# Sums over partitions by VectorE's 32x32 transposes instead of products with ones, in a hybrid attention and recurrence layer

## The chip, the cores and the metric

The kernel runs on one core of one Trainium2 chip. The metric is the device time of one execution in microseconds (us); several runs are taken and their median is given. In the profile PE is TensorE (PEld its weight loads), DVE is VectorE, ACT is ScalarE, POOL is GpSimd and SP is SyncE, which issues the transfers here.

## The reference

One decoder layer over 512 tokens of width 1024, in float32: x is normalised, one wide projection feeds a block-sparse attention branch (8 heads of 64) and a gated linear recurrence (4 heads of 128), and both are projected up, gated, merged and added to x. Two normalisations matter here, that of x over its 1024 channels and that of each recurrence head's output over its 128 channels:

```python
def rmsnorm(x, gain):
    xf = x.astype(jnp.float32)
    return xf * lax.rsqrt(jnp.mean(xf * xf, axis=-1, keepdims=True) + RMS_EPS) * gain.astype(jnp.float32)
...
xn = rmsnorm(h, norm_gain[i]).astype(dt)
proj = xn @ w_in[i]
aq, ak, av, ag, bq, bf, bi, bg, gate_a, gate_b = jnp.split(proj, split_pts, axis=-1)
...
yb = hgrn2_chunkwise(qb, kb, vb, log_f)
yb = rmsnorm(yb, hgrn_out_gain[i].reshape(HGRN_HEADS, HGRN_VDIM)).reshape(b, s, HGRN_WIDTH)
```

## The kernel before

**Layout.** x and the heads' outputs lie with channels on the 128 partitions and the 512 tokens on the free axis. x is eight tiles `xr0` to `xr7` of 128x512. A sum over channels is therefore a sum over partitions.

**Products.** To keep float32's precision, each operand is split into a high and a low part (`split`: ScalarE copies the high part, VectorE subtracts), and each product is three (`mm3`, line 256, and `proj_tok`, line 391). A weight matrix comes in pieces of 128x1024 (`wf`), each split into `wh` and `wl` (lines 239 and 240) two pieces ahead of use.

**Order.** TensorE runs in the order of the program. The main line is the list of projections: `bi` and `av` (values of the recurrence and of the attention, from x without its norm, `gh` and `gl`), then, with the normalised `xh` and `xl`, `bf0` and `bq0` (forget gate and query of recurrence head 0), `aq`, `ak`, and from `ORDER` the rest: `bg` and `ag` (gates), `bf`/`bq` 1 to 3, `gb` and `ga` (merge gates). The recurrence and the attention are generators that are woven into it: a counter `now` adds up an assumed cost of the products, and `yield 3.5` means that the generator goes on when 3.5 us more of products have been written. The order on VectorE, ScalarE, GpSimd and SyncE is set by a scheduler at build time, which takes what is marked with high priority sooner; each of these engines too runs its list strictly in order.

**x's norm.** While `bi` runs, the squares of the eight tiles are added into `ssum`. `x_norm` splits it, two products with `onesd` (1/1024 everywhere) put the mean of squares of each token on all partitions (`mp`), `rsqrt` takes the inverse root (logarithm and exponential on ScalarE, one step of Newton on VectorE, lines 267 to 272), and `xr` is scaled by it (line 355, three tiles on GpSimd). Four transposes (`mt`) turn it so that tokens are on partitions (`rt`), for the values.

**A recurrence head.** `hgrn_gates` prepares the gates; `hgrn_intra` prepares operands on VectorE and ScalarE (`hx`, `hkx`, `hqx`, last `near`, lines 463 to 465) and then has TensorE form the scores in small products (`lpb`, `lpa`); `hgrn_out` forms chunk states (`hktp`, `hds`, `st`) and the output (`hop`). Then comes the norm: the square `ht`, its split `hth` and `htl`, a pause of 3.5 us of products, two products with `ones128` (`hms`), `rsqrt`, and the scaling (line 609). The next head's `hgrn_intra` follows 3.1 us of products later, if its gates are there.

Of the kernel before, what the change touches and what calls it, by code (L numbers as in the profile page):

```python
# [12 lines left out]
R = mybir.dt.float32r  # L13
I32 = mybir.dt.int32
AF = mybir.ActivationFunctionType
OP = mybir.AluOpType
AX = mybir.AxisListType

S = 512
D = 1024  # L20
KD = D // 128
NT = S // 128
# [14 lines left out]
XN = 3.0  # L37
# [13 lines left out]
AHEAD = 150  # L51
# [6 lines left out]
def hybrid_layer_kernel(  # L58
# [16 lines left out]
    V, A, G, PE = nc.vector, nc.scalar, nc.gpsimd, nc.tensor  # L75

    cst = ctx.enter_context(tc.tile_pool(name="cst", bufs=1))
# [4 lines left out]


    BUFS = {"w": 2, "wh": 3, "wl": 3, "A": 16, "R": 4, "X": 16, "YB": 8, "H": 10, "T": 3, "Q": 4, "QM": 2, "QX": 2, "KT": 2, "P": 4, "PT": 2,
            "PT0": 2, "PT2": 2, "SG": 4, "YS": 1, "VV": 8, "s32": 1, "st": 1, "ps": 8}

    def unit(tag, name, dt=F32, shape=(128, 512)):
        return sb.tile(list(shape), dt, tag=tag, bufs=BUFS[tag], name=name)

    def bank(tag, name):  # L90
        return psum.tile([128, 512], F32, tag=tag, bufs={"mm": 4, "g": 2, "a": 2}[tag], name=name)
# [34 lines left out]
    def cost(us):  # L126
        now[0] += us
# [17 lines left out]
    one = nc.const_aps.tensor(1.0, (128, 128), F32)  # L145
    for i in range(WARM):
        PE.matmul(warm[:, 0:128], one, one, start=True, stop=True)
    onesd = cst.tile([128, 128], R, name="onesd")
    A.activation(onesd, one, AF.Copy, scale=1.0 / D)
    ones128 = cst.tile([128, 128], R, name="ones128")  # L150
    A.activation(ones128, one, AF.Copy, scale=1.0 / 128)
    epsc = cst.tile([128, 1], F32, name="epsc")
    V.memset(epsc, EPS)
    onec = cst.tile([128, 1], F32, name="onec")
# [1 line left out]
    ident = cst.tile([128, 128], F32, name="ident")  # L156
# [6 lines left out]
    ogain = sm[:, 10:14]  # L163
# [28 lines left out]
    def split(hi, lo, src):  # L192
        A.activation(hi, src, AF.Copy)
        V.tensor_tensor(lo, src, hi.bitcast(F32), op=OP.subtract)

    def scale_split(hi, lo, src, g):
        A.activation(hi, src, AF.Copy, scale=g)
        V.scalar_tensor_tensor(lo, src, g, hi.bitcast(F32), op0=OP.mult, op1=OP.subtract)
# [65 lines left out]

    def rsqrt(y, t, ms):

        A.activation(t, ms, AF.Ln, bias=epsc[:, 0:1])
        A.activation(y, t, AF.Exp, scale=-0.5)
        V.scalar_tensor_tensor(t, ms, EPS, y, op0=OP.add, op1=OP.mult)
        V.tensor_tensor(t, t, y, op=OP.mult)  # L270
        V.tensor_scalar(t, t, -0.5, 1.5, op0=OP.mult, op1=OP.add)
        V.tensor_tensor(y, y, t, op=OP.mult)
# [17 lines left out]
    rt = cst.tile([128, NT], F32, name="rt")  # L290
# [24 lines left out]
    ssum = unit("YB", "ssum")  # L315

    def x_square(k):
# [4 lines left out]
        A.activation(t, xr[k], AF.Square)  # L322
        V.tensor_tensor(ssum, ssum, t, op=OP.add)

    def x_norm():
        th = unit("YB", "ssh", R)
        tl = unit("YB", "ssl", R)
        with tc.high_priority(offset=AHEAD):
            split(th, tl, ssum)
        yield XN  # L330
        rstd = unit("YB", "rstd")
        with tc.high_priority(offset=AHEAD):
            x_normalise(th, tl, rstd)
        yield RT

        mt = bank("g", "mt")
        for t in range(NT):
            PE.transpose(mt[:, t * 128:t * 128 + 128], rstd[:, t * 128:t * 128 + 128], ident)
        cost(0.44)
        with tc.high_priority(offset=AHEAD):  # L340
            A.activation(rt, mt.rearrange("p (t n) -> p t n", t=NT)[:, :, 0], AF.Copy)
        for t in range(NT):
            A.activation(vb[t], vb[t], AF.Copy, scale=rt[:, t:t + 1])

    def x_normalise(th, tl, rstd):
        mp = bank("g", "mp")
        PE.matmul(mp, onesd, th, start=True, stop=False)
        PE.matmul(mp, onesd, tl, start=False, stop=True)
        cost(0.46)
        tmp = unit("YB", "rtmp")  # L350
        rsqrt(rstd, tmp, mp)
        with tc.manual_schedule(engines={mybir.EngineType.DVE}):
            def scaled(k):
                if k < KD and k not in ONPOOL:
                    V.scalar_tensor_tensor(xr[k], xr[k], gain[:, k:k + 1], rstd, op0=OP.mult, op1=OP.mult)
            for k in ONPOOL:
                G.tensor_tensor(xr[k], xr[k], rstd, op=OP.mult)
            scaled(0)
            scaled(1)
            for k in range(KD):  # L360
                h_ = unit("X", f"xh{k}", R)
                l_ = unit("X", f"xl{k}", R)
                if k in ONPOOL:
                    scale_split(h_, l_, xr[k], gain[:, k:k + 1])
                else:
                    split(h_, l_, xr[k])
                xh.append(h_)
                xl.append(l_)
                scaled(k + 2)


    def proj_tr(i, name):
        ws = weight(w_tr[i])
        ps = bank("mm", name)
        mm3(ps, ws[0], ws[1], xh, xl, KD)
        return ps
# [186 lines left out]
    def hgrn_out(h, vb):  # L563
        kb, qm, cum, kd = hg[h][:4]
        nk = 3 * 128
        yield 5.0
        kt = bank("g", f"hktp{h}")
        for c in range(3):
            PE.transpose(kt[:, c * 128:c * 128 + 128], kd[:, c * 128:c * 128 + 128], ident)
        cost(0.33)  # L570
        kts = unit("KT", f"hkt{h}", shape=(128, 3 * 128))
        A.activation(kts[:, :nk], kt[:, :nk], AF.Copy)
        yield 2.5
        hv = slice(h * 128, h * 128 + 128)
        dsp = bank("g", f"hds{h}")
        for c in range(3):
            PE.matmul(dsp[:, c * 128:c * 128 + 128], kts[:, c * 128:c * 128 + 128], vb[c][:, hv],
                      start=True, stop=True)
        cost(0.65)
        st = unit("st", f"st{h}", shape=(128, 3, 128))  # L580
        V.tensor_copy(st[:, 0], dsp[:, 0:128])
        for c in (1, 2):
            e = c * 128 + 127
            V.scalar_tensor_tensor(st[:, c], st[:, c - 1], cum[:, e:e + 1], dsp[:, c * 128:c * 128 + 128],
                                   op0=OP.mult, op1=OP.add)
        yield 3.0
        op_ = bank("g", f"hop{h}")
        for c in range(NT):
            s_ = slice(c * 128, c * 128 + 128)
            PE.matmul(op_[:, s_], vb[c][:, hv], sc[:, c, :], start=True, stop=(c == 0))  # L590
            if c:
                PE.matmul(op_[:, s_].rearrange("p (g t) -> p g t", t=32), st[:, c - 1], qm[:, 4 * c:4 * c + 4, 0:32],
                          start=False, stop=True)
        cost(1.5)
        o = unit("YB", f"ho{h}")
        y = unit("Q", f"hy{h}")
        t = unit("Q", f"ht{h}")
        th = unit("Q", f"hth{h}", R)
        tl = unit("Q", f"htl{h}", R)
        with tc.high_priority(offset=AHEAD):  # L600
            A.activation(t, op_, AF.Square)
            split(th, tl, t)
        yield 3.5
        ms = bank("g", f"hms{h}")
        PE.matmul(ms, ones128, th, start=True, stop=False)
        PE.matmul(ms, ones128, tl, start=False, stop=True)
        cost(0.43)
        rsqrt(y, t, ms)
        V.scalar_tensor_tensor(o, op_, ogain[:, h:h + 1], y, op0=OP.mult, op1=OP.mult)
        hg[h] += (o,)  # L610

    def hgrn_gated(h, sbg, res):
# [9 lines left out]
    def recurrence(vb, sbg, res):  # L622
        for h in range(GH):
            yield lambda: h in hg
            if h == 0:
                yield H0
            yield from hgrn_intra(h)
            yield from hgrn_out(h, vb)
            spawn(hgrn_gated(h, sbg, res))
            yield HP  # L630
# [215 lines left out]
    with tc.manual_schedule(engines=FIRST):  # L846
        bi = proj_tok(2, "bi", gh, gl, start)
    vb = values(bi, "bi")
    spawn(x_norm())
    va = values(proj_tok(3, "av", gh, gl), "av", rt)  # L850
    spawn(recurrence(vb, sbgs, yb))
# [11 lines left out]
    def up(i, n, ys, name):  # L863
        ws = weight(w_up[n, i])
        ps = bank("mm", name)
        mm3(ps, ws[0], ws[1], [y[0] for y in ys], [y[1] for y in ys], 4)
        return ps
# [3 lines left out]
    for kind, i in ORDER:  # L871
# [6 lines left out]
        elif kind == "ub":  # L878
            drain(f"yb{GH - 1}")
            ps = up(1, i, yb, f"ub{i}")  # L880
            V.tensor_tensor(sg["gb", i], ps, sg["gb", i], op=OP.mult)
        else:
            ps = proj_tr({"ga": 16, "gb": 24}[kind] + i, f"{kind}{i}")
# [3 lines left out]
    for n in range(KD):  # L887
        ga, gb = sg["ga", n], sg["gb", n]
        drain(f"ya{HPAIRS - 1}")
        ps = up(0, n, ya, f"ua{n}")  # L890
# [9 lines left out]
    for n in range(KD):  # L900
# [3 lines left out]
        ps = bank("mm", f"h{n}")  # L904
        mm3(ps, ws[0], ws[1], mh, ml, KD)
        t = unit("H", f"hf{n}")
# [8 lines left out]
    for k in range(2):  # L915
        t = unit("A", f"pf{k}")
# [6 lines left out]
    for n in range(KD):  # L923
# [10 lines left out]
        for i in range(parts):  # L934
# [8 lines left out]
            ps = bank("mm", f"g{n}_{i}")  # L943
# [3 lines left out]
            t = unit("Q", f"sg{n}_{i}")  # L947
# [71 lines left out]
```

## Time and profile before

| | |
|---|---|
| time, median of 3 runs | 469.99 us (469.82 to 1201.68) |
| the profiled execution | 469.64 us, its span 467.7 us |
| TensorE's granted clock | 0.999 of full speed |
| busy: PE, DVE, ACT, POOL | 462.7, 311.6, 274.6, 12.6 us |
| transfers | 50.42 MB, 108 GB/s on average |

The span runs from the first instruction to the last; the execution's own time also counts what lies around it. Rows of a timeline give start, duration, engine, line, operation and operands; a row of groups gives the busy time and the mean of one, then the idle time before them and what ended it.

### The profile page before, as it was taken

What the parts mean: (1) busy time and instruction counts of PE and PEld (TensorE: products, weight loads), DVE (VectorE), ACT (ScalarE), POOL (GpSimd) and SP (SyncE); (2) the same over time, 40 slices, a digit from 0 to 9 for tenths busy, and PEclk for the clock granted to TensorE, in tenths of its full rate; (3) what the DMA queues carried; (4) which work ended last, traced back from release to release, by engine and by line L of the source; (5) the groups of instructions that cost most, each with busy time, mean ns of one, the idle gap of its engine ahead of it and who ended that gap; (6) DMA issues with size and microseconds to landing.
All of it is one profiled execution on the core that took longest, in us unless ns stands there. A gap on an engine that the chain in (4) does not pass through costs nothing.

```text
span 467.7 us, 7249 instructions
## 1 busy us (share of the span) xinstructions
PE 462.7 (99%) x2776; PEld 385.2 (82%) x2776; DVE 311.6 (67%) x615; ACT 274.6 (59%) x479; POOL 12.6 (3%) x34
## 2 busy tenths in 40 slices
PE   9999999999999999999999999999999999999996
PEld 7888888888888888888888888888888888888886
DVE  4769668868979886978599556434559844544332
ACT  5866755668687987778687777455344522243201
POOL 0004000000000010000000000000000000000000
PEclk9999999999999999999999999999999999999999
DMA  7642223312363424131522242122534544322211
GB/s 246 213 138 90 92 93 108 114 46 91 116 133 115 134 57 135 61 111 48 157 90 71 89 135 69 46 68 69 179 91 135 202 148 163 97 90 90 92 45 46
DMA packets 19027, 50.42 MB, mean 108 GB/s; under 512 B 2352, under 2 KB 2992, under 8 KB 18992
## 3 DMA queue, kind: packets, MB, share of 16 engines
q1 hardware_dynamic: 18848, 49.95, 34.1%
q8 instruction: 22, 0.36, 0.3%
q14 instruction: 13, 0.11, 0.1%
q10 hardware_dynamic: 144, 0.01, 0.0%
HBM read 45.75 MB, written 2.10 MB: 102 GB/s over the span
## 4 chain that ended last, share of the span: by engine, by line
PE 95%; DVE 2%; ACT 1%; DMA 1%; SPq 0%; issue 0%; DVEq 0%
PE gb L256 9%; PE ga L256 9%; PE g L256 9%; PE h L256 9%; PE ua L256 5%; PE bq L256 5%; PE ub L256 5%; PE bf L256 5%; PE av L391 5%; PE aq L391 5%; PE ag L256 5%; PE bg L256 4%; PE bi L391 4%; PE ak L391 3%; PE pe L256 2%; PE s L704 2%
## 5 line engine op out<-in xcount | busy, mean ns | idle before, releaser
L239 ACT ACTIVATE wh<-wf 128x1024 fp32r<-128x1024 f32 (+1 forms) x78 | 75.8, 971 | 104.0 <-issue 20.1
L240 DVE TENSOR_TENSOR wl<-wf,wh 128x1024 fp32r<-128x1024 f32 (+1 forms) x78 | 87.7, 1126 | 49.9 <-ACT wh L239 47.3
L256 PE MATMUL g<-hh,wh 128*128 128x512 f32 (+1 forms) x72 | 26.3, 365 | 0.0
L256 PE MATMUL g<-hl,wh 128*128 128x512 f32 (+1 forms) x72 | 26.3, 365 | 0.0
L256 PE MATMUL g<-hh,wl 128*128 128x512 f32 (+1 forms) x72 | 26.3, 365 | 0.0
L256 PE MATMUL gb<-xh,wh 128*128 128x512 f32 x64 | 26.2, 410 | 0.0
L256 PE MATMUL ga<-xh,wh 128*128 128x512 f32 x64 | 25.6, 400 | 0.0
L256 PE MATMUL gb<-xh,wl 128*128 128x512 f32 x64 | 25.1, 392 | 0.0
L256 PE MATMUL gb<-xl,wh 128*128 128x512 f32 x64 | 25.0, 391 | 0.0
L256 PE MATMUL ga<-xh,wl 128*128 128x512 f32 x64 | 25.0, 391 | 0.0
L256 PE MATMUL ga<-xl,wh 128*128 128x512 f32 x64 | 25.0, 390 | 0.0
L256 PE MATMUL h<-mh,wh 128*128 128x512 f32 x64 | 24.9, 389 | 0.0
L256 PE MATMUL h<-ml,wh 128*128 128x512 f32 x64 | 24.9, 389 | 0.0
L256 PE MATMUL h<-mh,wl 128*128 128x512 f32 x64 | 24.9, 389 | 0.0
L713 ACT ACTIVATE p<-p,ps 128x128 f32<-128x128 f32 (+3 forms) x32 | 17.7, 552 | 5.8 <-DVE ps L711 5.8
L711 DVE CUSTOM_DVE_ANT_0 p<-s,bias 128x128 f32<-128x128 f32 (+3 forms) x32 | 15.0, 487 | 8.9 <-PE s L704 8.9
L726 ACT ACTIVATE ptS<-pt 128x384 f32<-128x384 f32 (+1 forms) x24 | 12.5, 522 | 11.3 <-PE pt L722 11.1
L907 DVE TENSOR_TENSOR hf<-h,xres 128x512 f32<-128x512 f32 x8 | 5.5, 692 | 18.3 <-PE h L256 18.3
L256 PEld LDWEIGHTS g<-hh,wl 128*128 128x128 f32 x72 | 13.6, 189 | 2.2
L256 PEld LDWEIGHTS g<-hh,wh 128*128 128x128 f32 x72 | 13.6, 189 | 2.2
L256 PEld LDWEIGHTS g<-hl,wh 128*128 128x128 f32 x72 | 13.6, 189 | 2.2
L949 DVE TENSOR_TENSOR sg<-sg,pe 128x512 f32<-128x512 f32 (+1 forms) x9 | 5.6, 625 | 14.4 <-ACT sg L948 12.0
(321 smaller groups left out, 1268.1 us busy)
## 6 DMA issues: line engine op xcount, KB each, us to landing
wf<-in_w_tr_dram SPq DMA_DIRECT2D x32, 512.0 KB, 3.3
wf<-in_w_tok_dram SPq DMA_DIRECT2D x15, 512.0 KB, 3.3
wf<-in_w_up_dram SPq DMA_DIRECT2D x16, 256.0 KB, 2.6
wf<-in_w_o_dram SPq DMA_DIRECT2D x8, 512.0 KB, 3.3
wf<-in_w_g_dram SPq DMA_DIRECT2D x8, 512.0 KB, 3.3
bias<-in_brow_dram SPq DMA_DIRECT2D x8, 256.0 KB, 3.5
xres<-in_xT_dram SPq DMA_DIRECT2D x8, 256.0 KB, 2.9
xr<-in_xT_dram SPq DMA_DIRECT2D x7, 256.0 KB, 4.9
```

Source lines behind the costliest of these rows:

```text
L239: A.activation(hi, wraw[i], AF.Copy)
L240: pin(V.tensor_tensor(lo, wraw[i], hi.bitcast(F32), op=OP.subtract))
L256: PE.matmul(ps, a[:, k, :], b[k], start=(n == 0), stop=(n == tot - 1))
L391: PE.matmul(banks[t], a[:, s_], b[:, kk, :], start=(k == 0 and i == 0), stop=(k == KD - 1 and i == 2))
L704: PE.matmul(sp[:, o:o + nk], qn[h][:, qs], k_[:, :nk], start=(i == 0), stop=(i == 1))
L711: V.tensor_tensor_reduce(p_, sp[:, o:o + nk], T[:, nk - 1::-1], -1.0, 3e38, OP.add, OP.min, st[:, 0:1])
L713: A.activation(p_, p_, AF.Exp, bias=st[:, 0:1], scale=-1.0, accum_out=st[:, 1:2])
L726: A.activation(pt, tp[:, :n * 128], AF.Copy)
L907: V.tensor_tensor(t, ps, xres, op=OP.add)
L949: V.tensor_tensor(t[:, :w], t[:, :w], pe[:, s_], op=OP.mult)
```

## The change

A helper `column_norms` takes the place of both sums. Its input is 128x512 of squares. `V.transpose` transposes every 32x32 block for itself, so that the free-axis sum over groups of 32 (`tensor_reduce`) adds up 32 channels: 128x16 partial sums, with a token's four quarters of channels on four groups of 32 partitions. Three additions bring them together on the first 32 partitions, where scaling and inverse root work on 32x16 instead of 128x512. The result is copied to the other three groups, spread 32 wide and transposed back, and so lies on all partitions, as before. `rt` is copied out of the small result instead of being transposed by TensorE. The two constant tiles and the pauses `XN` and 3.5 go.

```diff
-    onesd = cst.tile([128, 128], R, name="onesd")
-    A.activation(onesd, one, AF.Copy, scale=1.0 / D)
-    ones128 = cst.tile([128, 128], R, name="ones128")
-    A.activation(ones128, one, AF.Copy, scale=1.0 / 128)
...
+    def column_norms(src, n, name, tag):
+        u = unit(tag, name + "u")
+        sums = unit("n16", name + "s", shape=(128, 16))
+        y = unit("n16", name + "y", shape=(128, 16))
+        t_ = unit("n16", name + "t", shape=(128, 16))
+        g = [slice(32 * i, 32 * i + 32) for i in range(4)]
+        V.transpose(u, src)
+        V.tensor_reduce(sums, u.rearrange("p (b j) -> p b j", j=32), axis=AX.X, op=OP.add)
+        V.tensor_tensor(sums[g[0]], sums[g[0]], sums[g[1]], op=OP.add)
+        V.tensor_tensor(sums[g[2]], sums[g[2]], sums[g[3]], op=OP.add)
+        V.tensor_tensor(sums[g[0]], sums[g[0]], sums[g[2]], op=OP.add)
+        V.tensor_scalar(sums[g[0]], sums[g[0]], 1.0 / n, None, op0=OP.mult)
+        rsqrt(y[g[0]], t_[g[0]], sums[g[0]])
+        for i in range(1, 4):
+            V.tensor_copy(y[g[i]], y[g[0]])
+        z = unit(tag, name + "z")
+        V.tensor_copy(u.rearrange("p (b j) -> p b j", j=32), y[:, :, None].to_broadcast([128, 16, 32]))
+        V.transpose(z, u)
+        return y, z
...
     def x_norm():
-        th = unit("YB", "ssh", R)
-        tl = unit("YB", "ssl", R)
         with tc.high_priority(offset=AHEAD):
-            split(th, tl, ssum)
-        yield XN
-        rstd = unit("YB", "rstd")
-        with tc.high_priority(offset=AHEAD):
-            x_normalise(th, tl, rstd)
+            y, rstd = column_norms(ssum, D, "xn", "YB")
+            for g in range(4):
+                V.tensor_copy(rt[32 * g:32 * g + 32], y[0:32].rearrange("p (t g) -> p t g", g=4)[:, :, g])
+            x_normalise(rstd)
         yield RT
-        mt = bank("g", "mt")
-        for t in range(NT):
-            PE.transpose(mt[:, t * 128:t * 128 + 128], rstd[:, t * 128:t * 128 + 128], ident)
-        cost(0.44)
-        with tc.high_priority(offset=AHEAD):
-            A.activation(rt, mt.rearrange("p (t n) -> p t n", t=NT)[:, :, 0], AF.Copy)
...
         with tc.high_priority(offset=AHEAD):
             A.activation(t, op_, AF.Square)
-            split(th, tl, t)
-        yield 3.5
-        ms = bank("g", f"hms{h}")
-        PE.matmul(ms, ones128, th, start=True, stop=False)
-        PE.matmul(ms, ones128, tl, start=False, stop=True)
-        cost(0.43)
-        rsqrt(y, t, ms)
-        V.scalar_tensor_tensor(o, op_, ogain[:, h:h + 1], y, op0=OP.mult, op1=OP.mult)
+            y = column_norms(t, 128, f"h{h}n", "Q")[1]
+            V.scalar_tensor_tensor(o, op_, ogain[:, h:h + 1], y, op0=OP.mult, op1=OP.mult)
```

Three places show how the instructions stand on the engines. The first is TensorE in the middle of `av`, before the change:

```order
L391 MATMUL av2_336<-wh4_281,gl1_140 128x512
L391 MATMUL av2_336<-wl4_282,gh1_139 128x512
L347 MATMUL mp_367<-ssh_347,onesd_79 128x512
L348 MATMUL mp_367<-ssl_348,onesd_79 128x512
L391 MATMUL av3_337<-wh4_281,gh0_116 128x512
```

After it, the two products with ones are gone and `av` goes straight on; the four transposes `mt` and the four pairs `hms` are gone in the same way.

The second is VectorE at the norm of recurrence head 1 (`h1n...` are the helper's tiles, `p13` an attention tile, `hx2` operands of head 2). Before the change, the Newton steps on `ht1` stand between other work:

```order
L715 TENSOR_SCALAR p13_1840<-p13_1840,ps13_1841 128x512
L269 SCALAR_TENSOR_TENSOR ht1_1831<-hms1_1861,hy1_1830 128x512
L270 TENSOR_TENSOR ht1_1831<-ht1_1831,hy1_1830 128x512
L240 TENSOR_TENSOR wl31_1895<-wf31_1892,wh31_1894 128x1024
L450 TENSOR_TENSOR hx2_64_1922<-hu2_1721 128x4x64
L451 TENSOR_TENSOR hx2_64_1922<-hu2_1721 128x4x64
```

And after it:

```order
L708 TENSOR_SCALAR p13_1867<-p13_1867,ps13_1868 128x512
L333 TENSOR_TENSOR h1ns_1842<-h1ns_1842 32x16
L334 TENSOR_SCALAR h1ns_1842<-h1ns_1842 32x16
L265 SCALAR_TENSOR_TENSOR h1nt_1844<-h1ns_1842,h1ny_1843 32x16
L266 TENSOR_TENSOR h1nt_1844<-h1nt_1844,h1ny_1843 32x16
L267 TENSOR_SCALAR h1nt_1844<-h1nt_1844 32x16
L268 TENSOR_TENSOR h1ny_1843<-h1ny_1843,h1nt_1844 32x16
L337 COPY h1ny_1843<-h1ny_1843 32x16 x3
L339 COPY h1nu_1841<-h1ny_1843 128x512
L340 STREAM_TRANSPOSE h1nz_1860<-h1nu_1841 128x512
L452 TENSOR_TENSOR hx2_64_1891<-hu2_1730 128x4x64
L453 TENSOR_TENSOR hx2_64_1891<-hu2_1730 128x4x64
```

The whole small chain now stands as one piece ahead of head 2's `hx2`, and the split `wl31` has moved behind it.

The third is VectorE at `near`, the last operands of head 2's scores (`hq2`), before:

```order
L240 TENSOR_TENSOR wl34_2117<-wf34_2114,wh34_2116 128x1024
L463 TENSOR_TENSOR hq2_1737<-hu2_1721 128x16x16
L513 TENSOR_TENSOR hkd2_2151<-hu2_1721 128x384
L714 RECIPROCAL ps23_2099<-ps23_2099 128x1
L465 TENSOR_TENSOR hq2_1737<-hq2_1737 128x16x16
```

And after:

```order
L467 TENSOR_TENSOR hq2_1746<-hq2_1746 128x16x16
L517 TENSOR_TENSOR hkd2_2127<-hkd2_2127,hk2_1735 128x384
L708 TENSOR_SCALAR p22_2019<-p22_2019,ps22_2020 128x384
L190 TENSOR_TENSOR yal0_2094<-ya0_2091,yah0_2093 128x512
L704 ISA p23_2121,ps23_2122<-s23_2118,bias2_1427 128x512
L704 ISA ps23_2122 128x1
L236 TENSOR_TENSOR wl34_2141<-wf34_2138,wh34_2140 128x1024
```

The split `wl34`, which stood ahead of the pass on `hq2`, and `yal0` now stand behind it. On TensorE the scores `lpb2` that read it have moved from the products of `bq3` into those of `bf3`, three groups after its start.

More of the change, by code (lines that the diff above doesn't have):

```diff
@@ L84, in hybrid_layer_kernel @@
     BUFS = {"w": 2, "wh": 3, "wl": 3, "A": 16, "R": 4, "X": 16, "YB": 8, "H": 10, "T": 3, "Q": 4, "QM": 2, "QX": 2, "KT": 2, "P": 4, "PT": 2,
-            "PT0": 2, "PT2": 2, "SG": 4, "YS": 1, "VV": 8, "s32": 1, "st": 1, "ps": 8}
+            "PT0": 2, "PT2": 2, "SG": 4, "YS": 1, "VV": 8, "s32": 1, "st": 1, "ps": 8, "n16": 3}
     def unit(tag, name, dt=F32, shape=(128, 512)):
@@ L265, in rsqrt @@
     def rsqrt(y, t, ms):
-        A.activation(t, ms, AF.Ln, bias=epsc[:, 0:1])
+        A.activation(t, ms, AF.Ln, bias=epsc[0:t.shape[0], 0:1])
         A.activation(y, t, AF.Exp, scale=-0.5)
@@ L342, in x_norm, with x_normalise @@
+            for g in range(4):
+                V.tensor_copy(rt[32 * g:32 * g + 32], y[0:32].rearrange("p (t g) -> p t g", g=4)[:, :, g])
+            x_normalise(rstd)
+        yield RT
         for t in range(NT):
             A.activation(vb[t], vb[t], AF.Copy, scale=rt[:, t:t + 1])
[L345 to L351, printed above, removed]
+    def x_normalise(rstd):
@@ L595, in hgrn_out @@
         o = unit("YB", f"ho{h}")
-        y = unit("Q", f"hy{h}")
         t = unit("Q", f"ht{h}")
-        th = unit("Q", f"hth{h}", R)
-        tl = unit("Q", f"htl{h}", R)
         with tc.high_priority(offset=AHEAD):
             A.activation(t, op_, AF.Square)
-            split(th, tl, t)
-        yield 3.5
-        ms = bank("g", f"hms{h}")
-        PE.matmul(ms, ones128, th, start=True, stop=False)
-        PE.matmul(ms, ones128, tl, start=False, stop=True)
-        cost(0.43)
-        rsqrt(y, t, ms)
-        V.scalar_tensor_tensor(o, op_, ogain[:, h:h + 1], y, op0=OP.mult, op1=OP.mult)
+            y = column_norms(t, 128, f"h{h}n", "Q")[1]
+            V.scalar_tensor_tensor(o, op_, ogain[:, h:h + 1], y, op0=OP.mult, op1=OP.mult)
         hg[h] += (o,)
```

## The prediction

> **What bounds the kernel now.** I read the page's table of engines first, then the shares of the chain that ended last, then TensorE's waits.
>
> ```profile
> PE 462.7 (99%) x2776; PEld 385.2 (82%) x2776; DVE 311.6 (67%) x615; ACT 274.6 (59%) x479; POOL 12.6 (3%) x34
> ```
> ```profile
> PE 95%; DVE 2%; ACT 1%; DMA 1%; SPq 0%; issue 0%; DVEq 0%
> ```
> ```profile
> PE warm L147 <- PEq L1006: 0.8, 1, 0.8
> PE hms L606 <- DVE htl L194: 0.2, 1, 0.2
> ```
>
> TensorE is busy for 462.7 of 467.7 us, 95% of the chain is TensorE, and in the whole program it waited for another engine once: 0.2 us, for `htl`, an operand that this change removes. So the time is the length of TensorE's queue plus what others make it wait. An edit saves what it takes out of that queue and costs what it makes TensorE wait.
>
> Busy time is not the price of a product, since neighbours overlap. The price is the distance between starts, so I read the timeline around each product that goes: `mp` and `mt` of x's norm, `hms` of head 0 and of head 1 (start, duration, what).
>
> ```profile
> 31.62 0.39 PE L347 MATMUL mp<-ssh,onesd 128*128 128x512 f32 x1
> 31.86 0.39 PE L348 MATMUL mp<-ssl,onesd 128*128 128x512 f32 x1
> 32.08 0.40 PE L391 MATMUL av<-wh,gh 128*128 128x512 f32 x1
> ```
> ```profile
> 40.06 0.39 PE L391 MATMUL av<-wl,gh 128*128 128x512 f32 x1
> 40.29 0.60 PE L338 MATMUL mt<-ident,rstd 128*128 128x128 f32 x4
> 40.64 0.48 PE L391 MATMUL av<-wh,gh 128*128 128x512 f32 x1
> 40.96 0.40 PE L391 MATMUL av<-wh,gl 128*128 128x512 f32 x1
> ```
> ```profile
> 113.53 0.40 PE L256 MATMUL bg<-xh,wl 128*128 128x512 f32 x1
> 113.76 0.39 PE L605 MATMUL hms<-hth,ones 128*128 128x512 f32 x1
> 114.40 0.50 PE L606 MATMUL hms<-htl,ones 128*128 128x512 f32 x1 [0.25 <-DVE htl L194]
> 114.74 0.39 PE L256 MATMUL bg<-xh,wh 128*128 128x512 f32 x1
> ```
> ```profile
> 179.88 0.39 PE L605 MATMUL hms<-hth,ones 128*128 128x512 f32 x1
> 180.11 0.39 PE L606 MATMUL hms<-htl,ones 128*128 128x512 f32 x1
> 180.34 0.49 PE L722 MATMUL pt<-ident,p 128*128 128x128 f32 x3
> ```
>
> **What TensorE is spared.** Wide neighbours start 0.23 us apart (179.88 to 180.11). Without `mp`, the product at 32.08 stands where `mp` did: 32.08 - 31.62 = 0.46 us. Without the four transposes `mt`: 40.64 - 40.29 = 0.35, and the product behind them no longer takes 0.32 instead of 0.23 to the next start, 0.09 more: 0.44. Head 0's `hms`: 114.74 - 113.76 = 0.98, its wait included. Heads 1 to 3 go as head 1: 180.34 - 179.88 = 0.46, three times 1.38. Together 0.46 + 0.44 + 0.98 + 1.38 = 3.26 us.
>
> [...]
>
> The two constants made at the start (`onesd`, `ones128`) go too. They cost nothing today, since ScalarE's next instruction waits for a transfer:
>
> ```profile
> 3.21 0.51 ACT L197 ACTIVATE gh<-xr,sm 128x256 fp32r<-128x256 f32 x1 [0.24 <-DMA sm<-in_smalls_dram]
> ```
>
> **What the other engines get.** The groups of instructions by shape (busy us, mean ns, idle before):
>
> ```profile
> L194 DVE TENSOR_TENSOR htl<-ht,hth 128x512 fp32r<-128x512 f32 x4 | 2.8, 690 | 1.0 <-ACT hth L193 1.0
> L269 DVE SCALAR_TENSOR_TENSOR ht<-hms,hy 128x512 f32<-128x512 f32 x4 | 2.8, 693 | 8.8 <-ACT hy L268 8.8
> L270 DVE TENSOR_TENSOR ht<-ht,hy 128x512 f32<-128x512 f32 x4 | 2.8, 690 | 0.1
> L271 DVE TENSOR_SCALAR ht<-ht 128x512 f32<-128x512 f32 x4 | 1.7, 419 | 0.0
> L643 DVE TENSOR_REDUCE kss<-kq 128x8 f32<-128x512 f32 x4 | 2.7, 682 | 0.1
> L270 DVE TENSOR_TENSOR kt<-kt,ky 128x32 f32<-128x32 f32 x1 | 0.2, 186 | 0.0
> ```
> ```profile
> L193 ACT ACTIVATE hth<-ht 128x512 fp32r<-128x512 f32 x4 | 2.5, 631 | 0.1
> L267 ACT ACTIVATE kt<-kss,epsc 128x32 f32<-128x32 f32 x1 | 0.3, 310 | 0.0
> L268 ACT ACTIVATE ky<-kt 128x32 f32<-128x32 f32 x1 | 0.2, 217 | 0.0
> ```
>
> Per head VectorE loses `htl`, line 269, line 270 and a product like it, and line 271: 4 x 0.69 + 0.42 = 3.2 us. It gets a free-axis sum over 512 columns (0.68, like `kss`), a spreading copy (between the 0.42 of a one-source operation and 0.69; I take 0.55), eleven operations on 32x16 (at most 0.19 each, like `kt`: 2.1) and two 32x32 transposes, which no row shows. Their nearest rows are 0.42 and 0.69 for 512 columns; I take 0.69, the more usual. Sum 0.68 + 0.55 + 2.1 + 1.4 = 4.7, so **VectorE gets 1.5 us per head more**, 1.0 with the lower end. It should also lose most of the 8.8 / 4 = 2.2 us that it idles before line 269, because the logarithm and exponential shrink to 0.31 + 0.22 us and wait for no product.
>
> [...]
>
> All of this lies beside a full TensorE and is free so long as each operand is ready when TensorE reaches it. The slack is what counts, and I look at the two tightest places.
>
> **x's norm.** VectorE's rows of the old sum's split, of the scaling of x and of its last remainder, and TensorE's first product that reads them:
>
> ```profile
> 26.97 0.68 DVE L194 TENSOR_TENSOR ssl<-ssum,ssh 128x512 fp32r<-128x512 f32 x1
> ```
> ```profile
> 37.38 2.45 DVE L355 SCALAR_TENSOR_TENSOR xr<-xr,sm,rstd 128x512 f32<-128x512 f32 x2
> ```
> ```profile
> 50.85 0.69 DVE L194 TENSOR_TENSOR xl<-xr,xh 128x512 fp32r<-128x512 f32 x1
> ```
> ```profile
> 50.30 0.39 PE L256 MATMUL bf<-xh,wh 128*128 128x512 f32 x1
> ```
>
> The last remainder is ready at 51.54 and needed for the eighth group of three products, at 50.30 + 7 x 0.68 = 55.1: 3.5 us of slack. TensorE arrives 0.46 + 0.44 = 0.9 us sooner, leaving 2.6. The new chain has no products to wait for: 4.7 us of VectorE, 0.5 of ScalarE and four copies into `rt`, against 10.4 us from the split at 26.97, in whose place the order puts the first transpose, to 37.38. Even with a wait for a weight's split inside, I expect the scaling to begin 2 to 3 us sooner. The four scalings of the value tile now stand ahead of `xh` on ScalarE; the head start covers them. Nothing of it should show.
>
> **The scores of head 2 (`lpb2`).** The 3.5 us pause in the recurrence goes, so the next heads' products come sooner. Today's rows are the last product of head 1's output, the last pass of VectorE's work for head 2 (`near`, line 465), and the scores; the last line is a step of four short attention products from the chain:
>
> ```profile
> 175.74 0.39 PE L592 MATMUL hop<-hq,st 128*128 128x128 f32 x2
> ```
> ```profile
> 182.16 0.69 DVE L269 SCALAR_TENSOR_TENSOR ht<-hms,hy 128x512 f32<-128x512 f32 x1 [2.93 <-ACT hy L268]
> ```
> ```profile
> 204.05 1.23 DVE L240 TENSOR_TENSOR wl<-wf,wh 128x1024 fp32r<-128x1024 f32 x1 [0.66 <-ACT wh L239]
> ```
> ```profile
> 206.16 0.43 DVE L465 TENSOR_TENSOR hq<-hq 128x256 f32<-128x256 f32 x1
> ```
> ```profile
> 211.39 0.43 PE L526 MATMUL lpb<-hx 128*32 128x64 f32 x16
> ```
> ```profile
> 156.85 0.46 PE s L704 x4
> ```
>
> Slack today: 211.39 - 206.59 = 4.8 us. In the changed order 26 fewer wide products stand between `hop1` and `lpb2` (102 instead of 128), and three transposes (0.3 by `mt`'s row) and four short products (0.5) fewer: 26 x 0.23 + 0.8 = 6.8 us less room. VectorE gains 0.6 (no `hth`) and 2.3 (0.6 of waiting in place of 2.93), pays 1.5, and has `wl34` and `yal` behind the pass instead of ahead of it: 1.2 + 0.7. Slack left: 4.8 - 6.8 + 0.6 + 2.3 - 1.5 + 1.9 = **1.3 us**. Head 3 today:
>
> ```profile
> 257.72 0.43 DVE L465 TENSOR_TENSOR hq<-hq 128x256 f32<-128x256 f32 x1
> ```
> ```profile
> 262.97 0.43 PE L526 MATMUL lpb<-hx 128*32 128x64 f32 x16
> ```
>
> Its slack is 262.97 - 258.15 = 4.8 too, but only 17 wide products and six short ones go between `hop2` and `lpb3`, about 4.8 us; with credits of the same kind (3.3) it keeps about 3. So no stall, but this is where one would be.
>
> **Sum.** The profiled execution took 469.64 us, 467.7 of it the span. 469.64 - 3.26 = 466.4; the median of the runs, 469.99, lies 0.35 above that execution, so I predict **466.7 us**, 0.7% less. A change under 2% is about what a measurement of this kernel can't tell from none.
>
> **Rivals.**
> 1. *Part of the gain is given back* by sub-microsecond waits at moved products: `lpb2`, the probability transpose right behind it, the keys. For: the slack of 1.3 us is a difference of terms that are each good to half a microsecond, and VectorE is 67% busy. Against: TensorE waits once today. 467.6 to 469.6.
> 2. *VectorE becomes the bound of the recurrence: slower.* If a transpose takes much over 0.69 us, `near` is late for `lpb2`, then for `lpb3`, and TensorE stands. Each microsecond more per transpose costs 2 per head, so the slack of 1.3 is gone at 1.3 us per transpose and that of 3 at 2.2. At 3 us each, `lpb2` waits 4.6 - 1.3 = 3.3 and `lpb3` 1.6, more than the 3.26 saved: 471. It turns slower than before from 2.6 us per transpose on, four times the nearest row. Against: every row of VectorE over 512 columns lies under 1 us unless GpSimd works beside it (2.45 us for two at 37.38).
> 3. *TensorE isn't the bound where the products go*: the weights' splits pace it, and the time freed returns as waiting. For: VectorE and ScalarE, which split them, are 67% and 59% busy. Against: TensorE's waits name no weight. 469.6.
> 4. *More is gained* than the queue holds: nothing but waiting could give it, and there is almost none. Under 465.6.
>
> **How the numbers follow.** Forecast 0.68 (465.8 to 467.6); rival 1 0.17; rival 2 0.08; rival 3 0.04; rival 4 0.03. The range 465.6 to 469.7 holds the forecast and rivals 1 and 3, and the transposes' bounds of 0.42 to 0.69 us. Faster by over 2% needs under 460.4: 0.02. Slower by over 2% needs over 479, a transpose of some 5 us: 0.02.
>
> **What would show it.** Right: TensorE's busy time near 459.5, no wait of it that names `hx`, `hq` or `xl`, transposes near 0.7 us, `bf` beginning near 49.4. Wrong: a row of TensorE's waits on VectorE in the recurrence, transposes over 1.3 us, or gaps before `lpb`.

## The result, and the profile after

The changed kernel takes **472.81 us** (median; 472.31 to 473.39), beside 469.96 before on the same chip: a ratio of 1.0062, 95% interval 1.0042 to 1.0082. One run before took 1201.68 us; the ratio leaves it out. The change is 2.85 us slower where 3.26 less was forecast; some 6 us have to be found. The engines of the page and the chain's shares after:

```profile
PE 465.4 (99%) x2762; PEld 382.7 (81%) x2762; DVE 317.4 (67%) x669; ACT 267.0 (57%) x471; POOL 13.1 (3%) x34
```
```profile
PE 96%; DVE 1%; DMA 1%; SPq 0%; ACT 0%; issue 0%; DVEq 0%
```

TensorE has 14 products fewer and is busy 2.7 us longer. TensorE's waits after:

```profile
PE warm L147 <- PEq L999: 0.8, 1, 0.8
PE pt L715 <- DVE p L708: 0.3, 1, 0.3
PE bi L393 <- ACT wh L189: 0.2, 1, 0.2
```

Half a microsecond in all, so the loss isn't waiting. It is in the distance between starts. In the last stage, the final projection, the edit changes no instruction, only addresses: 24 products `g` and 6 products `pe` alternate. Rows of TensorE's timeline of before, the first of group 1 and the first of group 7 of `g`, 180 products apart:

```profile
410.24 0.39 PE L256 MATMUL g<-hh,wh 128*128 128x512 f32 x1
...
451.04 0.39 PE L256 MATMUL g<-hh,wh 128*128 128x512 f32 x1
```

And the same two after:

```profile
412.17 0.39 PE L252 MATMUL g<-hh,wh 128*128 128x512 f32 x1
...
454.13 0.39 PE L252 MATMUL g<-hh,wh 128*128 128x512 f32 x1
```

40.80 us became 41.96: 0.2267 us per product became 0.2331, while each row's duration stays 0.39. The stage before it, `h` (`mh` by `wh`), doesn't do this. Its rows of before, 168 products apart:

```profile
365.36 0.39 PE L256 MATMUL h<-mh,wh 128*128 128x512 f32 x1
...
403.44 0.39 PE L256 MATMUL h<-mh,wh 128*128 128x512 f32 x1
```

And after:

```profile
367.27 0.39 PE L252 MATMUL h<-mh,wh 128*128 128x512 f32 x1
...
405.35 0.39 PE L252 MATMUL h<-mh,wh 128*128 128x512 f32 x1
```

38.08 us both times, 0.2267. What sets the stages apart is the operand: all that got slower, `pe` apart, read `xh`, `xl` (`bf`, `bq`, `aq`, `ak`, `bg`, `ag`, `gb`, `ga`) or `hh`, `hl` (`g`). These four names share one pool of 16 tiles, tag X. The three new tiles of 128x16 (`n16`, 3 x 64 bytes per partition) are allocated just ahead of that pool. In the built programs the first bytes of the tiles within a partition are, modulo 2048:

| | `wh`, `wl`, the tiles A (`gh`, `ml`, ...) and `mh` | X | X minus `wh`, modulo 512 |
|---|---|---|---|
| before | 704 | 704 | 0 |
| after | 1728 | 1920 | 192 |

`pe` fits in: it reads no X, but its weights `pwh` and `pwl` are allocated behind X and moved with it, from 0 to 192 bytes past its other operands (`ph`, `pl`, tiles A) modulo 512, and its distance went from 0.2267 to 0.2319 us.

So **theory A**: a product's distance to the next depends on where its two operands lie relative to each other. **Theory B**: VectorE's or ScalarE's new work (its traffic or its order) slows TensorE.

### The profile page after: what moved, and what is told of

Read it like the earlier page. It is cut to its first block, busy times and chain, and to the rows that moved or that the text cites. A ratio compares the mean times of both kernels' runs of the same rounds, so it can differ in the third digit from the quotient of the medians.

```text
span 470.6 us, 7271 instructions
## 1 busy us (share of the span) xinstructions
PE 465.4 (99%) x2762; PEld 382.7 (81%) x2762; DVE 317.4 (67%) x669; ACT 267.0 (57%) x471; POOL 13.1 (3%) x34
## 4 chain that ended last, share of the span: by engine, by line
PE 96%; DVE 1%; DMA 1%; SPq 0%; ACT 0%; issue 0%; DVEq 0%
PE ga L252 10%; PE g L252 9%; PE h L252 9%; PE gb L252 9%; PE ak L393 5%; PE bg L252 5%; PE bq L252 5%; PE bf L252 5%; PE aq L393 5%; PE ag L252 5%; PE ua L252 5%; PE ub L252 5%; PE av L393 5%; PE bi L393 4%; PE pe L252 2%; PE s L697 2%
## 5 line engine op out<-in xcount | busy, mean ns | idle before, releaser
L236 DVE TENSOR_TENSOR wl<-wf,wh 128x1024 fp32r<-128x1024 f32 (+1 forms) x78 | 87.3, 1120 | 49.4 <-ACT wh L235 48.9
```

What stands on the lines that cost most here:

```text
L236: pin(V.tensor_tensor(lo, wraw[i], hi.bitcast(F32), op=OP.subtract))
```

## The experiments

In all that follow, "distance" is the mean of the distance between the starts of neighbouring wide products, for those that read X, `pe` counted with them (some 1,080 pairs), and for the others (`bi`, `av`, `ub`, `ua` and `h`, some 560), from the timeline; pairs over 0.26 us apart are left out, since something else stands between them.

**1. The helper tiles 512 bytes wide**, nothing else:

```diff
-        sums = unit("n16", name + "s", shape=(128, 16))
+        sums = unit("n16", name + "s", shape=(128, 128))[:, 0:16]
```
(and `y`, `t_` alike)

> The changed kernel, only with its three 32x16 helper tiles (`n16`) allocated 512 bytes wide per partition instead of 64. They are allocated just ahead of the 16 tiles that hold the halves of x and of the recurrence's output (tag X: xh, xl, hh, hl), so the X tiles go from 192 bytes to 0 bytes past a multiple of 512 relative to the weights' tiles wh and wl; no instruction changes. Theory A (addresses): wide products that read X start 0.233 us apart in the changed kernel and 0.227 before because of that shift; here 0.227 returns in bf, bq, aq, ak, bg, ag, gb, ga and g, the saved 3.26 us show, and the time is 466.4 to 467.0. Theory B (the new work on VectorE and ScalarE, its memory traffic or its order, slows TensorE): nothing changes, 472.8 +- 0.7.

Measured: **468.02 us**, ratio to before 0.9956 (0.9941 to 0.997). Its engines, waits, and `g`:

```profile
PE 459.8 (99%) x2762; PEld 382.7 (82%) x2762; DVE 317.0 (68%) x669; ACT 266.8 (57%) x471; POOL 13.1 (3%) x34
```
```profile
PE pt L715 <- DVE p L708: 1.2, 2, 0.7
PE warm L147 <- PEq L999: 0.8, 1, 0.8
```
```profile
408.54 0.39 PE L252 MATMUL g<-hh,wh 128*128 128x512 f32 x1
...
449.34 0.39 PE L252 MATMUL g<-hh,wh 128*128 128x512 f32 x1
```

40.80 us again. TensorE is busy 5.6 us less than in the changed kernel, with the same instructions in the same order. Theory B falls. The changed kernel's own trace speaks against it too. In this stretch of `g` (window, length, then busy time and count of PE, PEld, DVE, ACT and POOL, the granted clock, the transfers' busy share and GB/s) VectorE, ScalarE and GpSimd do nothing, and yet the products start 0.2332 us apart:

```profile
455.10:459.40 4.30, 4.30 (x20) 3.47 (x19) 0.00 (x0) 0.00 (x0) 0.00 (x0) 1.00 0.16 61
```

The time of experiment 1 is 1 us above the theory's range, and the waits say why: 1.2 us for the probabilities `p` (experiments 4 and 5).

**2. The kernel before with 192 unused bytes ahead of X**:

```diff
+        gap = sb.tile([128, 48], F32, tag="gap", bufs=1, name="gap")
+        V.memset(gap[:, 0:1], 0.0)
```

> The kernel before, only with an unused 192-byte tile (written once, one element) allocated just ahead of the X tiles, so that X lies 192 bytes past a multiple of 512 relative to wh and wl. Theory A (addresses): the products that read X start 0.233 us apart instead of 0.227, about 1152 products times 0.0055 = 6.3 us, so 475.5 to 477; bi, av, ub, ua and h, which don't read X, stay at 0.227. Theory B (the change's own work slows TensorE): 470.0 +- 0.5, distances as before.

Measured: 475.35 us, ratio 1.0111 (1.0096 to 1.0126). Its engines and `g`:

```profile
PE 468.1 (99%) x2776; PEld 385.0 (81%) x2776; DVE 312.1 (66%) x616; ACT 274.5 (58%) x479; POOL 12.6 (3%) x34
```
```profile
414.82 0.39 PE L256 MATMUL g<-hh,wh 128*128 128x512 f32 x1
...
456.78 0.39 PE L256 MATMUL g<-hh,wh 128*128 128x512 f32 x1
```

41.96 us for 180 products, as in the changed kernel, and 5.4 us more of TensorE's time, without any of the change. The price per product was set a little high: 0.0053 us on average, not 0.0055.

**3. Which address counts?** First everything is moved by 192 bytes together (experiment 1, with the unused tile among the constants).

> As e1_pad512, with a further unused 192-byte tile among the constants ahead of everything, so that X, wh, wl and the tiles A all move by 192 bytes and keep their distances to each other (0 modulo 512). Theory A1 (what counts is the address of one operand relative to the other): 0.227 us in every stage, 466.4 to 467.0. Theory A2 (what counts is where a tile lies by itself): 0.233 in the stages that read X, and also in bi, av, ub, ua and h, whose tiles now lie as X lies in the changed kernel: 472 to 477. Theory B (the change's own work): 472.8.

Measured: 467.99 us, ratio 0.9958 (0.9944 to 0.9972), like experiment 1; distances 0.2278 and 0.2271. So it is not the address by itself (A2 falls). Then eight offsets in one kernel:

```diff
-                h_ = unit("X", f"xh{k}", R)
-                l_ = unit("X", f"xl{k}", R)
+                h_ = unit("XH", f"xh{k}", R, (128, 528))[:, 0:512]
+                l_ = unit("XL", f"xl{k}", R, (128, 528))[:, 0:512]
```

> As e1_pad512, with X split into eight tiles XH (high halves) and eight XL (low halves), each 64 bytes longer than its 2048, so that xh and xl of feature tile k lie 64 k bytes past a multiple of 512 relative to wh and wl, k = 0 to 7. One trace gives the distance between starts by offset 0, 64, 128, ... 448. Theory A1 (relative offset): 0.227 for k = 0 and 0.233 for k = 3, the others tell the rule (only k = 0; all multiples of 128; or a slope); by the share of offsets that are slow the time lies between 467 and 473. Theory B (the change's own work): no difference between the k, 0.233 throughout, 472.8.

Measured: 471.89 us in one run, distance 0.2315. The separation by k failed: in `g` the eight gave 0.2314, 0.2324, 0.2300, 0.2286, 0.2329, 0.2329, 0.2300, 0.2289, even k = 0 not at 0.227. A product's distance seems to depend on its neighbours' offsets too, which this run can't separate, so the next three kernels give all products one offset, as experiment 2 does, with 64, 128 and 256 bytes:

> The kernel before with an unused tile of 64 bytes ahead of the X tiles (e2_before192 with 64 in place of 192): X lies 64 bytes past a multiple of 512 relative to wh and wl. Read is the distance between starts of the wide products that read X. If only 0 modulo 512 is fast: 0.233 us, 475 to 476. If offsets below some size are fast, or a multiple of 64 is: 0.227, 470.

> As b_gap64 with 128 bytes. If only 0 modulo 512 is fast: 0.233 us, 475 to 476. If every multiple of 128 is: 0.227, 470.

> As b_gap64 with 256 bytes. If only 0 modulo 512 is fast: 0.233 us, 475 to 476. If every multiple of 256 is: 0.227, 470.

At last the weights alone are moved off all others:

```diff
+        gap = sb.tile([128, 48], F32, tag="gap", bufs=1, name="gap") if i == 0 else None
         hi = unit("wh", f"wh{i}", R, (128, 2, 512))
         lo = unit("wl", f"wl{i}", R, (128, 2, 512))
+        if i == 0:
+            gap2 = sb.tile([128, 80], F32, tag="gap2", bufs=1, name="gap2")
```
(each written once, one element)

> The kernel before, with an unused 192-byte tile ahead of wh and wl and an unused 320-byte tile behind them: the weights' halves move by 192 bytes, X by 512, the tiles A (gh, mh, ml and their like) stay. Now the weights lie off a multiple of 256 from every other operand: A minus wh is -192, X minus wh is 320, both 64 modulo 256. Theory A1 (the distance of the two operands modulo 256, whatever the tile): the products that don't read X slow down too, for the first time (bi, av, ub, ua and h from 0.227 to between 0.229 and 0.233 us, as with offsets of 64 and 192), and those that read X go to 0.231 as in b_gap64: 475 to 479. Theory A2 (only where X itself lies): 0.227 everywhere, 470.

Measured, one run each for the gaps of 64, 128 and 256 and for the last; by stage the mean over whole groups of three products (`bf` is that of head 0):

| X minus `wh` | time, us | TensorE busy, us | reads X | others | `bf` | `aq` | `g` | `h` | `bi` |
|---|---|---|---|---|---|---|---|---|---|
| 0 (before) | 469.96 | 462.7 | 0.2278 | 0.2273 | 0.2267 | 0.2277 | 0.2267 | 0.2267 | 0.2283 |
| 64 | 473.21 | 466.4 | 0.2307 | 0.2275 | 0.2296 | 0.2333 | 0.2313 | 0.2268 | 0.2277 |
| 128 | 474.68 | 467.7 | 0.2326 | 0.2274 | 0.2333 | 0.2332 | 0.2330 | 0.2269 | 0.2276 |
| 192 (experiment 2) | 475.35 | 468.1 | 0.2331 | 0.2273 | 0.2333 | 0.2333 | 0.2333 | 0.2270 | 0.2277 |
| 256 | 469.88 | 463.0 | 0.2280 | 0.2274 | 0.2267 | 0.2278 | 0.2267 | 0.2271 | 0.2279 |
| weights moved (320) | 473.88 | 467.0 | 0.2300 | 0.2305 | 0.2296 | 0.2333 | 0.2289 | 0.2289 | 0.2332 |

Offsets of 0 and 256 bytes are fast, 64, 128 and 192 are not: "only 0 modulo 512" falls, as does "every multiple of 64" or of 128. That 64 costs only half as much as 192 was in no theory; its time and that of 128 came 1.8 and 0.3 us below the range for a slow offset. With the weights moved, `h` and `bi`, which never read X, slow down for the first time. The rows of `h` there, again 168 products apart:

```profile
368.99 0.39 PE L256 MATMUL h<-mh,wh 128*128 128x512 f32 x1
...
407.45 0.39 PE L256 MATMUL h<-mh,wh 128*128 128x512 f32 x1
```

38.46 us instead of 38.08. So it is the distance of the two operands (A1), not tag X. `pe`, whose operands stay 0 apart there, stays at 0.227. That run came 1 us below its range, because an offset of 64 costs differently in different stages (`aq` 0.2333, `bf` 0.2296). The stages differ in which operand is loaded as the 128x128 block and which is read with 512 columns. In `bi`, `av`, `aq` and `ak` (`proj_tok`) the block comes from x's tile, and these took 0.232 to 0.2335 at every slow offset. In the projections of `mm3` the block comes from the weights: they took 0.229 to 0.231 where the other operand lay 64 bytes (modulo 256, as here) past the weights (`pe` after the change: 0.232), and 0.2333 at 192. Why the role matters, these runs don't tell.

**4. The two halves of the change alone**, helper tiles padded as in experiment 1. The edits put back the old lines of the heads (then of `x_norm`).

> The change at x's norm alone (the recurrence's norms as before, by products with ones), with the helper tiles 512 bytes wide so that X stays at 0 modulo 512 from wh and wl. Theory A (what is saved is TensorE's queue, 0.46 + 0.44 = 0.90 us): 469.0 to 469.2 beside 469.94 before. Rival C (part of that comes back as waits of TensorE at the first product that reads x): 469.5 to 470.

> The change at the four recurrence norms alone (x's norm as before), helper tiles 512 bytes wide. TensorE's queue is spared 0.98 + 3 x 0.46 = 2.36 us. Theory A2 (the two waits for the probabilities p at 197 and 248 us, 1.2 us in e1_pad512, come from VectorE's added work per head): waits of about 1.2 us show here too, gain 2.36 - 1.2 = 1.2 us, 468.7 to 469.0. Rival C (they come from x's part, by TensorE being ahead): no such waits, gain 2.3 us, 467.6.

Measured: x alone 469.24 us (0.9985; 0.9976 to 0.9994), just above theory A's range, heads alone 468.65 (0.9973; 0.9963 to 0.9982), before 469.89. The gains of 0.65 and 1.24 us add up to 1.89, and experiment 1 gained 1.92. TensorE's waits with the heads alone:

```profile
PE pt L733 <- DVE p L726: 1.2, 2, 0.7
PE warm L147 <- PEq L1017: 0.8, 1, 0.8
PE bi L411 <- ACT wh L191: 0.2, 1, 0.2
```

The waits for `p` belong to the heads, and 2.36 - 1.2 = 1.16 agrees with 1.24. For x 0.25 us are missing from 0.90; that trace has a wait of 0.6 us at the very first product, for a weight's split that the change doesn't touch. But the stage that this product opens ends only 0.2 us later than before (`av` begins at 27.72 instead of 27.54), so that is at most part of the reason, and the rest stays open.

**5. Less on VectorE.** Why `p` is late is seen in two windows of experiment 1 that end about where the waits do (columns as in the window of experiment 1):

```profile
180.00:197.30 17.30, 16.65 (x109) 13.82 (x107) 17.15 (x45) 15.15 (x28) 0.45 (x2) 1.00 0.19 65
230.00:248.50 18.50, 17.94 (x116) 14.91 (x114) 18.50 (x46) 15.30 (x30) 0.43 (x2) 1.00 0.25 87
```

VectorE is busy for 35.65 of 35.80 us. In the same windows before it was 30.31:

```profile
180.00:197.30 17.30, 17.30 (x106) 14.44 (x106) 15.11 (x37) 14.17 (x26) 0.43 (x2) 1.00 0.19 64
230.00:248.50 18.50, 18.50 (x105) 15.36 (x105) 15.21 (x37) 13.37 (x24) 0.45 (x2) 1.00 0.25 72
```

And its queue in experiment 1 ahead of the first wait shows what `p` stands behind, with TensorE's wait last:

```profile
194.86 1.22 DVE L236 TENSOR_TENSOR wl<-wf,wh 128x1024 fp32r<-128x1024 f32 x1
196.00 0.44 DVE L465 TENSOR_TENSOR hq<-hu 128x256 f32<-128x256 f32 x1
196.33 0.57 DVE L515 TENSOR_TENSOR hkd<-hu 128x384 f32<-128x384 f32 x1
196.80 0.56 DVE L708 TENSOR_SCALAR p<-p,ps 128x128 f32<-128x128 f32 x2
...
197.25 0.61 PE L715 MATMUL pt<-ident,p 128*128 128x128 f32 x3 [0.65 <-DVE p L708]
```

The edit to experiment 1, for the heads:

```diff
-            A.activation(t, op_, AF.Square)
+            A.activation(t, op_, AF.Square, scale=128 ** -0.5)
...
-        V.tensor_scalar(sums[g[0]], sums[g[0]], 1.0 / n, None, op0=OP.mult)
+        if n == D:
+            V.tensor_scalar(sums[g[0]], sums[g[0]], 1.0 / n, None, op0=OP.mult)
...
-        V.tensor_copy(u.rearrange("p (b j) -> p b j", j=32), y[:, :, None].to_broadcast([128, 16, 32]))
+        ub_, yb_ = u.rearrange("p (b j) -> p b j", j=32), y[:, :, None].to_broadcast([128, 16, 32])
+        if n == D:
+            V.tensor_copy(ub_, yb_)
+        else:
+            A.activation(ub_, yb_, AF.Copy)
```

> e1_pad512 with some 0.65 us less on VectorE per head: the copy that spreads the norm to 128x512 goes to ScalarE (0.43 us), and the division by 128 is a scale of ScalarE's square (0.16 us and a start). Same sums otherwise. If TensorE's waits of 0.65 and 0.56 us for the probabilities are VectorE's queue being that much too long, both shrink to 0.2 us or less and the time is 466.6 to 467.2. If they come from something else (ScalarE's exponentials of the scores, or order), they stay or grow and the time is 468.0 or more.

Measured: **466.63 us**, ratio 0.9934 (0.9921 to 0.9946), the fastest of all. Engines and waits:

```profile
PE 459.4 (99%) x2762; PEld 382.8 (82%) x2762; DVE 314.5 (68%) x661; ACT 268.7 (58%) x475; POOL 13.1 (3%) x34
```
```profile
PE warm L147 <- PEq L1004: 0.8, 1, 0.8
PE pt L720 <- DVE p L713: 0.5, 1, 0.5
```

The time came as expected, the waits only in part: the second is gone, the first went only from 0.65 to 0.5, since the scheduler again put a `wl` ahead of `p`. In the profiled executions the span fell by 1.3 us. Of these, 0.7 are the waits; 0.5 lie in `bi` and ahead of it, before anything that this edit touches (`av` begins at 27.29 instead of 27.76). So about half of the gain over experiment 1 is shown to come from VectorE.

## Why the prediction was wrong, point by point

- **The step that failed** is the one on which the sum rests: "An edit saves what it takes out of that queue and costs what it makes TensorE wait." It leaves out that the products that stay can change their own length. "Wide neighbours start 0.23 us apart" was read before and carried over; for the two thirds of them whose operands had moved apart it became 0.2331 instead of 0.2278. No rival had this step either: all four deal with waits. In profiled executions: 469.64 - 3.26 (queue) + 5.6 (distance; TensorE busy 465.4 beside 459.8 in experiment 1) + 0.5 (two new waits) = 472.5; measured 472.75.
- **The 3.26 us themselves were right** to within a few tenths. TensorE's busy time was to be near 459.5; with the tiles padded it is 459.8 and 459.4. That the change saves this was hidden in its own result by a loss almost twice as large.
- **What a measurement can tell**: a change under 2% was called hard to tell from none. The interval of the ratio here spans 0.4%, and it tells 0.6% from none.
- **x's norm**: `bf` was to begin near 49.4. From the timelines after, TensorE's first `bf` and VectorE's scaling of x:

```profile
49.35 0.39 PE L252 MATMUL bf<-xh,wh 128*128 128x512 f32 x1
```
```profile
33.45 2.45 DVE L357 SCALAR_TENSOR_TENSOR xr<-xr,sm,xnz 128x512 f32<-128x512 f32 x2
```

  The scaling begins 3.9 us sooner than at 37.38; 2 to 3 were expected.
- **The transposes**, which no row of before showed, and the spreading copy, from the groups by shape after:

```profile
L329 DVE STREAM_TRANSPOSE h0nu<-ht 128x512 f32<-128x512 f32 x1 | 0.7, 700 | 0.0
L340 DVE STREAM_TRANSPOSE h2nz<-h2nu 128x512 f32<-128x512 f32 x1 | 0.7, 714 | 0.1
L339 DVE COPY h2nu<-h2ny 128x512 f32<-128x512 f32 x1 | 0.4, 429 | 0.0
L331 DVE TENSOR_TENSOR h1ns<-h1ns 32x16 f32<-32x16 f32 x1 | 0.2, 164 | 0.0
```

  0.70 to 0.71 us, against 0.69 taken; the copy 0.43 against 0.55, the small operations 0.16 to 0.17 against at most 0.19. VectorE got 1.1 us per head more (heads alone: busy 315.9 against 311.6), not 1.5.
- **Rival 1 had the right kind of wait, but not its place.** It named "the probability transpose right behind" `lpb2`; the two that waited with the tiles padded, at 197.25 and 248.30 us, stand ahead of `lpb2` and `lpb3`. What made them late was VectorE's full queue and not `near`: with the tiles padded, `near` of head 2 ends at 199.52 + 0.44 = 199.96 and `lpb2` starts at 203.72, a slack of 3.8 us where 1.3 was worked out. In the changed kernel only 0.3 of the 1.2 us show; there, behind the slower products, the first of the two starts at 199.56 us instead of 197.25. Padded, the time of 468.02 lies in that rival's 467.6 to 469.6.
- **Rival 2**, the slower side, has nothing to do with the slower time: it needed transposes of 2.6 us. **Rival 3** falls too: in the changed kernel TensorE waits for a weight's split once, 0.2 us, at the start.

## What to carry to other kernels

An edit that allocates a tile, even 192 bytes, moves what is allocated after it: compare the addresses of the operands of the products in both built programs before summing up what the instructions cost. Where the engine that bounds has no waits and yet gets busier with fewer instructions, compare the distances between starts by stage, and then by the tiles that the stages read. Helper tiles padded so that the pools behind them stay at 0 bytes modulo 512 from the weights' gave back 4.8 us of 473 here (472.81 to 468.02); a gap of 256 bytes in the kernel before cost nothing (469.88 beside 469.96).

## What the runs showed of the hardware that was not expected

Wide products with split operands started 0.2267 us apart in `bf` and `g` where their two operands lay 0 or 256 bytes apart modulo 512. In `bf`, `aq` and `g` they started 0.229 to 0.233 us apart at 64 and 320, and 0.233 at 128 and 192: up to 3% more per product. Moving both together by 192 bytes changed nothing (experiment 3: 0.2278 and 0.2271 on average). A row's printed duration, 0.39 in both kernels, hides it: in `g` the median is 389 ns before and 394 after. What it is in the relative address that costs the time, no run here shows.
